# A two-layer transformer step: the MLP up-projection by seven block products per pair of tiles, in place of eight

## The chip, the cores and the metric

The kernel runs on one core of one Trainium2 chip, with fp32 data split into two fp32r parts. The metric is the device time of one launch in microseconds (us). TensorE (PE) multiplies, VectorE (DVE), ScalarE (ACT) and GpSimd (POOL) do the elementwise work, and all transfers are issued in order by SyncE (SP).

## The reference

Two layers (DEPTH 2) work on 128 context and 512 latent tokens of width 1024; the kernel lays them out as 640 token columns. Cut to what matters here:

```python
mod = silu(cvec) @ w_ada[l] + b_ada[l]            # 6144 wide: sh1, sc1, g1, sh2, sc2, g2
h = x * (1 + sc1) + sh1
...                                               # three branches, gated merge, w_out
x = layer_norm(ALPHA * x + g1 * mixed, ln1_g, ln1_b)
h = x * (1 + sc2) + sh2
f = square(relu(h @ w_up[l])) @ w_down[l]         # 1024 -> 4096 -> 1024
x = layer_norm(ALPHA * x + g2 * f, ln2_g, ln2_b)
```

## The kernel before

The program is recorded in Python order and then placed on each engine's queue by a scheduler at build time; each queue runs in order. All matrix products are made of 128x128 weights and 320 or 256 moving columns. For precision each operand is a pair (hi, lo), and each product has three matmuls: hi·hi, hi·lo, lo·hi. `split` makes the pair: ScalarE copies x to hi (L241), VectorE takes lo = x - hi (L242).

The MLP (`mlp`) has 32 up tiles of 128 hidden columns in four pieces (pc) of eight. `fm_blocks` loads the 1024x128 weight of a tile as two halves of 128x512, splits them into a ring of three hi and three lo buffers (`WB`), and `mm_fm` (L163) makes 2 token halves x 8 k-blocks x 3 = 48 matmuls of 128x320 of them. The results go through ReLU (L1212) and square (L1213) and are split again. Then the piece's eight tiles are multiplied into the 1024 outputs (`mm_tm`, L207, four column blocks of 120 matmuls of 128x256, added up in five y tiles at L1243). Hidden tiles of even and odd pieces lie in two sets of sixteen buffers (`even16`, `odd16`). The last piece first scales y by g2 (L1206, GpSimd) and adds ALPHA·x (L1207).

The modulation vector is made in 12 blocks (cb) of 512 columns per layer by `ada_block`: eight weight loads of 256 KB, each multiplied into two accumulators (`acc`), then four matmuls that sum over partitions (L319), a bias and a trip through DRAM (`modd`). Blocks 0 to 3 are sh1 and sc1, 4 and 5 are g1, 6 to 9 are sh2 and sc2, 10 and 11 are g2. `ada_in` does it with two weight buffers and two accumulators in the buffers `F6` and `qs`, with the second accumulator's work on ScalarE and GpSimd (L306, L308); `ada` does it on VectorE alone (L312). In layer 0, blocks 6 to 9 run by `ada_in` beside the gates and merges (`gates`, `merge_a`, `merge_b`, `merge_c`; L163 into `br`); blocks 10 and 11 and all twelve of layer 1 run by `ada` in the MLP of layer 0. Layer 1 has no such work. After the merges comes `out_proj` (L207 again, from `wout`).

## Time and profile before

| | |
|---|---|
| runs | 2985.76 us median of 3 (2978.71 to 2990.69) |
| profiled execution | 2984.24 us, span 2982.3 us |
| TensorE busy | 2790.9 us, 94% of the span, 21248 matmul records |
| VectorE, ScalarE, GpSimd busy | 1958.2, 1366.9, 680.4 us |
| mean granted TensorE clock | 0.956 of full speed |

The profiled execution lasts 1.9 us longer than its span, which begins with its first instruction. Stretches are told by times from the span's start: the MLP of layer 0 runs from about 1048 to 1530 us, that of layer 1 from about 2518 to 2971 us.

### The profile page before, as it was taken

The numbers are of one execution on the slowest core, as the hardware profiler recorded it, in microseconds if no ns is written. First come the engines' busy times: TensorE is split into PE (matmuls) and PEld (weight loads), VectorE is DVE, ScalarE is ACT, GpSimd is POOL, SyncE is SP. The second block draws the span as 40 slices with busy tenths as digits, with TensorE's granted clock in tenths as the row PEclk, the third lists the DMA queues.
The fourth block names the chain that finished last, engine by engine and source line by source line (L and its number), as shares of the span: only waits on it lengthen the run. The fifth ranks groups of instructions, "written<-read, shape, count | busy, mean of one in ns | idle before, by whom it ended". The sixth has DMA issues, their size and how long they took to land.

```text
span 2982.3 us, 56431 instructions
## 1 busy us (share of the span) xinstructions
PE 2790.9 (94%) x21248; PEld 2529.0 (85%) x21248; DVE 1958.2 (66%) x3824; ACT 1366.9 (46%) x3206; POOL 680.4 (23%) x869
## 2 busy tenths in 40 slices
PE   7989989999978999999989899799999899999998
PEld 5979877887868889999989788687878798999998
DVE  4686877877776776777474878878676466223346
ACT  3445665565652343332344456655655424342332
POOL 3241271312233300001040312713121014000011
PEclk8989989999989999999999899899999999999999
DMA  7534323343478244545235433333433762222242
GB/s 261 183 109 118 100 85 92 98 111 87 122 251 260 96 146 148 151 148 184 93 112 154 115 113 95 101 95 93 115 90 91 229 225 89 71 75 75 75 132 85
DMA packets 331255, 378.37 MB, mean 127 GB/s; under 512 B 158111, under 2 KB 180119, under 8 KB 330983
## 3 DMA queue, kind: packets, MB, share of 16 engines
q1 hardware_dynamic: 330983, 374.77, 41.1%
q8 instruction: 167, 2.74, 0.4%
q14 instruction: 105, 0.86, 0.1%
HBM read 306.83 MB, written 67.83 MB: 126 GB/s over the span
## 4 chain that ended last, share of the span: by engine, by line
PE 62%; DVE 15%; DMA 11%; ACT 5%; issue 4%; SPq 2%; POOL 1%; DVEq 0%; ACTq 0%; POOLq 0%
PE tm L207 17%; PE fm L163 16%; PE gl L163 7%; PE br L163 3%; PE tm L233 2%; PE uA L163 2%; PE g L820 2%; DVE Pm L861 2%; DVE T L862 2%; SPq L125 2%; PE st L974 1%; PE xp L939 1%; DVE lo L242 1%; PE ada L319 1%; PE tx L928 1%
## 5 line engine op out<-in xcount | busy, mean ns | idle before, releaser
L242 DVE TENSOR_TENSOR lo<-raw,hi 128x512 fp32r<-128x512 f32 x514 | 383.6, 748 | 401.2 <-ACT hi L241 395.2
L163 PE MATMUL fm<-h,hi 128*128 128x320 f32 (+1 forms) x2720 | 614.6, 315 | 13.3 <-ACT h L391 10.1
L241 ACT ACTIVATE hi<-raw 128x512 fp32r<-128x512 f32 x514 | 323.0, 630 | 612.2 <-PE tm L207 311.8
L163 PEld LDWEIGHTS fm<-h,hi 128*128 128x128 f32 x2720 | 462.7, 192 | 32.1 <-issue 11.2
L163 PE MATMUL fm<-h,lo 128*128 128x320 f32 (+2 forms) x1360 | 421.0, 315 | 9.0 <-DVE lo L242 9.0
L163 PE MATMUL gl<-h,hi 128*128 128x320 f32 x1536 | 379.2, 325 | 2.7 <-ACT f L1002 2.7
L163 PEld LDWEIGHTS gl<-h,hi 128*128 128x128 f32 x1536 | 266.2, 193 | 22.1 <-issue 11.0
L163 PEld LDWEIGHTS fm<-h,lo 128*128 128x128 f32 x1360 | 259.1, 192 | 13.6 <-DVE lo L242 10.2
L163 PE MATMUL gl<-h,lo 128*128 128x320 f32 x768 | 249.1, 325 | 1.8 <-DVE lo L242 1.8
L861 DVE TENSOR_TENSOR Pm<-T,ab 120x341 f32<-120x341 f32 (+30 forms) x434 | 174.2, 401 | 9.1
L862 DVE TENSOR_TENSOR T<-T,Pm 120x341 f32<-120x341 f32 (+30 forms) x434 | 172.8, 398 | 9.4
L312 DVE SCALAR_TENSOR_TENSOR acc<-P,c_sg,acc 128x512 f32<-128x512 f32 x196 | 142.9, 770 | 44.8 <-DMA P<-in_wada_dram 43.5
L1206 POOL TENSOR_TENSOR X<-X,e 128x512 f32<-128x512 f32 x8 | 11.5, 1442 | 680.3 <-DMA e<-modd 355.8
L207 PE MATMUL tm<-hi,h 128*128 128x256 f32 x800 | 160.3, 294 | 0.0
L163 PEld LDWEIGHTS gl<-h,lo 128*128 128x128 f32 x768 | 148.1, 193 | 8.6 <-issue 2.3
L163 PE MATMUL br<-h,hi 128*128 128x320 f32 x512 | 125.9, 334 | 19.7 <-DVE Q L1037 8.2
L207 PEld LDWEIGHTS tm<-hi,h 128*128 128x128 f32 x800 | 130.2, 196 | 5.2 <-issue 1.6
L978 ACT ACTIVATE q1k<-st,edge 64x64 f32<-64x64 f32 x320 | 98.6, 308 | 72.7 <-PE st L974 66.7
L207 PE MATMUL tm<-hi,L 128*128 128x256 f32 x720 | 131.8, 283 | 0.0
L537 POOL TENSOR_TENSOR P<-P,Q 128x512 f32<-128x512 f32 x64 | 84.2, 1316 | 170.9 <-PE o L535 66.8
L207 PE MATMUL tm<-lo,h 128*128 128x256 f32 x400 | 116.7, 292 | 4.5 <-DVE lo L242 4.5
L163 PEld LDWEIGHTS br<-h,hi 128*128 128x128 f32 x512 | 91.3, 201 | 31.2 <-issue 15.8
(554 smaller groups left out, 6899.0 us busy)
## 6 DMA issues: line engine op xcount, KB each, us to landing
raw<-in_win_f_dram SPq DMA_DIRECT2D x172, 256.0 KB
raw<-in_wup_dram SPq DMA_DIRECT2D x128, 256.0 KB
raw<-in_wdn_dram SPq DMA_DIRECT2D x128, 256.0 KB
P<-in_wada_dram SPq DMA_DIRECT2D x114, 256.0 KB
w<-rk SPq DMA_DIRECT2D x48, 321.5 KB
...
```

The costliest lines, as they stand in the source:

```text
L125: self.nc.sync.dma_start(out=out, in_=in_)
L163: nc.tensor.matmul(ps.at(h), w[:, c], ps.of(h, x), start=(k == 0 and p == 0), stop=(k == n - 1 and p == 2))
L207: nc.tensor.matmul(out[t], x[:, ts], w[:, c], start=(k == 0 and p == 0 and (alone or t < 2)), stop=(k == n - 1 and p == 2 and (alone or t ...
L233: nc.tensor.matmul(o, x[:, ts], w[:, c], start=(k == 0 and p == 0), stop=(k == n - 1 and p == 2))
L241: self.nc.scalar.activation(hi, x, AF.Copy)
L242: self.nc.vector.tensor_sub(lo, x, hi.bitcast(F32))
L312: nc.vector.scalar_tensor_tensor(acc[:, s], w, cs[:, k, s:s + 1], acc[:, s], ALU.mult, ALU.add)
L537: nc.gpsimd.tensor_tensor(out=den, in0=den, in1=PT, op=ALU.add)
L820: nc.tensor.matmul(pg[h][:, 128 * j:128 * j + 128], BK[pr, c0 + j].rearrange("p s t -> p (s t)"), RAV[pr, c0 + j, 0:2, :].rearrange("p s t ...
L861: eng.tensor_tensor(out=p, in0=T[:, :, i:i + 1].to_broadcast(sh), in1=Am[:, i, js].unsqueeze(1).to_broadcast(sh), op=ALU.mult)
L862: eng.tensor_tensor(out=T[:, :, js], in0=T[:, :, js], in1=p, op=ALU.add)
L978: nc.scalar.activation(St[kr, s, h, :], p4[kr, s, h, :], AF.Copy, scale=edge[kr, cc:cc + 1])
```

## The change

Tiles 0 to 3 of each layer are made as before. The other 28 are made in 14 pairs (`pair`, `seven`). The product of a pair is seen as a 2x2 block product (two tiles; two halves of k; two halves of the tokens), which is made by seven block products and sums in place of eight. Each block product has 4 k-blocks x 3 = 12 matmuls of 128x320, so 84 for a pair. For it GpSimd takes four differences of weight halves per pair, each of the seven weight operands is split, and VectorE adds the seven results into f0 and f1 out of PSUM. Four sums and differences of blocks of h (`s1` to `s4`) are made and split once per layer by `seven_x`. The lo part of the hidden tiles moves from VectorE to GpSimd (`part`). Hidden tiles lie in a ring of five groups of four buffers, one group a pair (`ring4`): "20 tiles". Weight halves get up to three raw buffers more. One pair of the next piece is made ahead of each piece's output product.

The adaLN blocks 4 to 9 of layer 1 move from the MLP of layer 0 to layer 1's gates and merges (`ada_in`), blocks 10 and 11 of layer 1 to the MLP of layer 1 (`ada`). The scaling of the layer's first norm (`res_tail`) is recorded after pair 2. The scaling of y by g2 is recorded beside pairs 13 to 15.

```diff
+    def ring4(self, n, dt=F32R):
+        n %= 5
+        if n < 3:
+            return [self.K(t, dt)[:, 0:NTOK] for t in K13[4 * n:4 * n + 4]]
...
+    def seven_x(self, g, L, tmp):
...
+        whole(1, 0, nc.vector)
+        whole(0, 0, nc.gpsimd)
+        whole(1, 1, nc.vector)
+        tt((1, 1), (1, 0), (1, 1), ALU.add)
+        parts((1, 1), s1)
+        tt((1, 1), (1, 1), (0, 0), ALU.subtract)
+        parts((1, 1), s2)
+        whole(0, 1, nc.gpsimd)
+        tt((1, 0), (0, 0), (1, 0), ALU.subtract)
+        parts((1, 0), s3)
+        tt((0, 1), (0, 1), (1, 1), ALU.subtract)
+        parts((0, 1), s4)
...
+        def prod(raw, x):
...
+            self.split(raw, hi, lo)
+            ps = bank()[:, 0:HALF]
+            for q in range(4):
+                c = slice(128 * q, 128 * q + 128)
+                for p, (w, i) in enumerate(((hi, 0), (hi, 1), (lo, 0))):
+                    nc.tensor.matmul(ps, w[:, c], x(q, i), start=(q == 0 and p == 0), stop=(q == 3 and p == 2))
...
+        sub = lambda o, a, b: nc.gpsimd.tensor_tensor(out=o, in0=a, in1=b, op=ALU.subtract)
+        add = lambda o, ps, b: nc.vector.tensor_tensor(out=o, in0=ps, in1=b, op=ALU.add)
...
+        nc.scalar.activation(fa, prod(b11, ops["a11"]), AF.Copy)
+        sub(b11, b12, b11)
+        sub(b12, b22, b12)
+        m3 = prod(b22, ops["s4"])
+        sub(b22, b22, b11)
+        add(fb, prod(b22, ops["s2"]), fa)
+        add(ga, m3, fb)
+        add(fa, prod(b21, ops["a12"]), fa)
+        sub(b21, b21, b22)
+        add(gb, prod(b12, ops["s3"]), fb)
+        add(fb, prod(b21, ops["a22"]), gb)
+        last()
+        m5 = prod(b11, ops["s1"])
+        add(ga, m5, ga)
+        add(gb, m5, gb)
...
+            def part(f, hi, lo):
+                nc.scalar.activation(hi, f, AF.Copy)
+                nc.gpsimd.tensor_tensor(out=lo, in0=f, in1=hi.bitcast(F32), op=ALU.subtract)
+
+            def last():
+                nc.scalar.activation(f0, f0, AF.Relu)
+                nc.scalar.activation(f0, f0, AF.Square)
+                part(f0, s[0], s[1])
+
+            self.seven(up(2 * n), up(2 * n + 1), ops, f0, f1, bank, raws, last)
+            nc.vector.scalar_tensor_tensor(f1, f1, 0.0, f1, ALU.max, ALU.mult)
+            part(f1, s[2], s[3])
...
+            while n < 4 * pc + 5 and n < 16:
+                pair(n)
+                if end:
+                    scale(((0, 1), (2, 3), (4,))[n - 13])
+                n += 1
...
-            if l == 0:
...
-                side = self.ada_in([(0, cb) for cb in range(4 + EARLY, 10)], F6[:, 0:2], [F6[:, 2], self.big1("qs", [128, 512])])
...
+            side = self.ada_in([(l, cb) for cb in range(4 if l else 4 + EARLY, 10)], F6[:, 0:2], [F6[:, 2], self.big1("qs", [128, 512])])
...
-            todo = [(0, 10), (0, 11)] if l == 0 else []
...
+            todo = [(l, 10), (l, 11)]
...
-                todo += [(l + 1, cb) for cb in range(12)]
...
+                todo += [(l + 1, cb) for cb in range(4)]
```

ScalarE's queue in an up stage of layer 1, before: L241 with hi<-raw splits a weight half, L1212 and L1213 are ReLU and square of a tile, L241 with L<-f its hi part.

```order
L1212 ACTIVATE f_29973<-fm_29923 128x320
L241 ACTIVATE hi_29987<-raw_29985 128x512
L241 ACTIVATE hi_30049<-raw_30047 128x512
L1212 ACTIVATE f_29973<-fm_29924 128x320
L1213 ACTIVATE f_29973<-f_29973 128x640
L241 ACTIVATE L_29704<-f_29973 128x640
```

ScalarE's queue after, in layer 1 where pair 7 (Q_30437 is its f0, Q_30438 its f1) hands over to pair 8 (f_30586): L321 splits a weight half, L1309, L1310 and L1305 are ReLU, square and hi part, L253 takes the first product of a pair out of PSUM.

```order
L321 ACTIVATE hi_30593<-X_29142 128x512
L321 ACTIVATE hi_30613<-qs_29146 128x512
L1309 ACTIVATE Q_30437<-Q_30437 128x640
L1310 ACTIVATE Q_30437<-Q_30437 128x640
L1305 ACTIVATE ec_30433<-Q_30437 128x640
L253 ACTIVATE f_30586<-u_30597 128x320
L1305 ACTIVATE bon_30435<-Q_30438 128x640
L321 ACTIVATE hi_30631<-qs_29146 128x512
L321 ACTIVATE hi_30650<-raw_30591 128x512
L321 ACTIVATE hi_30669<-F_29144 128x512
```

Where weight halves stood between the ReLUs one or two at a time, the weights of pair 8's third product (hi_30631) now stand behind pair 8's first product and pair 7's last hi part.

GpSimd's queue in layer 1 at the last piece, before: after the first norm's scaling (L1168) nothing stands but the ten scalings of y by g2 (L1206) and then the norm.

```order
L1168 TENSOR_TENSOR y_27661<-y_27661,row_27664 128x512
L1206 TENSOR_TENSOR X_28534<-X_28534,e_32029 128x512
L1206 TENSOR_TENSOR X_28534<-X_28534,e_32031 128x512
L1206 TENSOR_TENSOR BK_28535<-BK_28535,e_32031 128x512
...
L1206 TENSOR_TENSOR y_28537<-y_28537,e_32032 128x512
L290 TENSOR_SCALAR rsd_33072<-mv_33070 128x1
```

The same place after: L249 are the weight differences (the first three and the fourth of pair 13, then those of pair 14), L1341 the scalings, L1306 the lo parts.

```order
L249 TENSOR_TENSOR raw_32558<-raw_32560,raw_32558 128x512
L249 TENSOR_TENSOR raw_32560<-raw_32560,qs_29146 128x512
L1341 TENSOR_TENSOR X_29142<-X_29142,e_32545 128x512
L1341 TENSOR_TENSOR X_29142<-X_29142,w_32546 128x512
L1341 TENSOR_TENSOR X_29142<-X_29142,w_32547 128x512
L1341 TENSOR_TENSOR BK_29143<-BK_29143,w_32547 128x512
...
L1341 TENSOR_TENSOR y_29145<-y_29145,Ld_32548 128x512
L249 TENSOR_TENSOR raw_32562<-raw_32562,raw_32560 128x512
L249 TENSOR_TENSOR X_29142<-F_29144,X_29142 128x512
```

All ten scalings now stand between the third and the fourth weight difference of pair 13.

SP's queue at the end of layer 1's merges, before: Q<-part and P<-gate are the last loads of the merges, wout the weights of the product after them.

```order
L125 DMA Q_27489<-part_3_209 128x640
L125 DMA P_27506<-gate_20_194 128x640
L125 DMA raw_27694<-in_wout_dram 128x512
L125 DMA Q_27566<-part_4_210 128x640
L125 DMA P_27536<-gate_21_195 128x640
```

The same place after, with F and qs the two weight buffers of the adaLN blocks.

```order
L129 DMA raw_27995<-in_wout_dram 128x512
L129 DMA qs_24909<-in_wada_dram 128x512
L129 DMA F_24908<-in_wada_dram 128x512
L129 DMA qs_24909<-in_wada_dram 128x512
L129 DMA F_24908<-in_wada_dram 128x512
L129 DMA qs_24909<-in_wada_dram 128x512
L129 DMA F_24908<-in_bada_r_dram 1x512 x2
L129 DMA qs_27795<-in_ln_b_dram 128x512
L129 DMA Q_27699<-part_4_210 128x640
L129 DMA Q_27704<-part_5_211 128x640
```

The loads of part tiles 4 to 7 now stand behind the last weights of the sixth adaLN block.

## Rows read from the trace of the kernel before

**Rows 1.** The page's parts 1 and 2: busy time, slices of the span.
```profile
PE 2790.9 (94%) x21248; PEld 2529.0 (85%) x21248; DVE 1958.2 (66%) x3824; ACT 1366.9 (46%) x3206; POOL 680.4 (23%) x869
...
PEclk8989989999989999999999899899999999999999
DMA  7534323343478244545235433333433762222242
```
**Rows 2.** Windows, L163 alone: stretch, length, PE and PEld busy, clock, DMA share, GB/s.
```profile
2626.00:2682.30 56.30, 56.30 (x384) 56.21 (x384) 1.00 0.22 71
...
2852.80:2914.00 61.20, 58.12 (x384) 57.72 (x384) 0.97 0.35 108
```
**Rows 3.** Groups by form, 2620 to 2800 us: busy us, mean ns, idle before.
```profile
L242 DVE TENSOR_TENSOR lo<-raw,hi 128x512 fp32r<-128x512 f32 x51 | 35.3, 692 | 102.6 <-ACT hi L241 102.6
L241 ACT ACTIVATE hi<-raw 128x512 fp32r<-128x512 f32 x51 | 32.3, 633 | 80.5 <-PE tm L207 49.9 <-PE fm L163 30.7
L1212 ACT ACTIVATE f<-fm 128x320 f32<-128x320 f32 x32 | 13.7, 430 | 27.6 <-PE fm L163 27.6
L1213 ACT ACTIVATE f<-f 128x640 f32<-128x640 f32 x16 | 11.8, 738 | 0.5
L242 DVE TENSOR_TENSOR L<-f,L 128x640 fp32r<-128x640 f32 x6 | 5.0, 825 | 7.1 <-ACT L L241 7.1
```
**Rows 4.** Groups by form, GpSimd, whole span.
```profile
L537 POOL TENSOR_TENSOR P<-P,Q 128x512 f32<-128x512 f32 x64 | 84.2, 1316 | 170.9 <-PE o L535 66.8 <-ACT Q L532 53.8 <-ACT f L1002 21.1
...
L1057 POOL TENSOR_TENSOR f<-f,Q 128x640 f32<-128x640 f32 x16 | 28.4, 1788 | 65.1 <-DVE Q L1037 43.3 <-DMA f<-part 21.7
```
**Rows 5.** Line L1037, VectorE from PSUM: duration ns min/median/max, first and last start.
```profile
L1037 DVE SCALAR_TENSOR_TENSOR Q<-Q,br x32: 471/484/489, 891.7 to 2411.0; 128x320 f32<-128x320 f32 x32
```
**Rows 6.** Timeline of GpSimd, 1403 to 1409.5 us: start, length, what.
```profile
1404.88 1.73 POOL L1206 TENSOR_TENSOR BK<-BK,e 128x512 f32<-128x512 f32 x1
1406.58 1.75 POOL L1206 TENSOR_TENSOR F<-F,e 128x512 f32<-128x512 f32 x1
```
**Rows 7.** Timeline of VectorE, 1403 to 1412.6 us.
```profile
1405.39 3.48 DVE L242 TENSOR_TENSOR lo<-raw,hi 128x512 fp32r<-128x512 f32 x2
1408.79 1.78 DVE L312 SCALAR_TENSOR_TENSOR acc<-P,c_sg,acc 128x512 f32<-128x512 f32 x1
...
1411.94 0.41 DVE L1243 TENSOR_TENSOR X<-tm,X 128x256 f32<-128x256 f32 x1
```
**Rows 8.** Timeline of TensorE, 1224 to 1229 us.
```profile
1224.98 1.02 PE L319 MATMUL ada<-acc,c_blk 128*1 128x512 f32 x2
1225.93 0.56 PE L163 MATMUL fm<-h,hi 128*128 128x320 f32 x2
```
**Rows 9.** Timelines of ScalarE and TensorE: one place in layer 0 and in layer 1.
```profile
780.69 0.44 ACT L990 ACTIVATE so<-fs 64x64 f32<-64x64 f32 x2
...
2272.86 0.44 ACT L990 ACTIVATE so<-fs 64x64 f32<-64x64 f32 x2
...
964.97 0.36 PE L207 MATMUL tm<-hi,e 128*128 128x256 f32 x1 [0.33 <-DVE P L1037]
...
2437.31 0.28 PE L207 MATMUL tm<-hi,e 128*128 128x256 f32 x1
```
**Rows 10.** Issues of the adaLN weights, 795 to 940 us: ns min/median/max, first and last.
```profile
L125 SPq DMA_DIRECT2D qs<-in_wada_dram x16: 328/333/447, 800.7 to 920.9; - x16
```
**Rows 11.** Windows, all engines: PE, PEld, DVE, ACT, POOL, clock, DMA share, GB/s.
```profile
900.00:965.00 65.00, 56.70 (x360) 53.41 (x358) 41.21 (x67) 17.23 (x27) 24.94 (x15) 0.97 0.84 264
```
**Rows 12.** Timelines at the start of layer 1's MLP: VectorE, TensorE.
```profile
2518.55 3.01 DVE L392 TENSOR_TENSOR h<-f,h 128x512 fp32r<-128x512 f32 x2
...
2542.47 0.31 PE L163 MATMUL fm<-h,lo 128*128 128x320 f32 x1
```
**Rows 13.** Last piece of layer 0: the chain that ended last; TensorE's timeline.
```profile
1399.09 4.59 DMA e<-modd
...
1423.62 0.63 PE L163 MATMUL fm<-h,lo 128*128 128x320 f32 x1 [4.02 <-DVE lo L242]
```

More of the change, by code (lines that the diff above doesn't have):

```diff
@@ L1160, in res_end, with res_tail @@
             self.res_norm(r, t, hT, sb, dst)
-        if hT is None:
-            return
+        if hT is not None and r.which:
+            self.res_tail(r, dst)
+    def res_tail(self, r, dst):
+        nc = self.nc
         for t in range(NT):
@@ L1173, in out_proj @@
         r = self.res_start(l, 0, xsrc)
-        self.res_rows(r, xsrc)
+        L, b = self.L([128, 4, 512]), self.big.tile([128, 2, 512], F32, tag="ab", name=self.nm("row"))
+        self.res_rows(r, [L[:, i] for i in range(4)] + [b[:, 0], b[:, 1], r.more[0], r.more[2]],
+                      ((0, "m"), (1, "m"), ("ln1", "_g"), ("ln1", "_b")))
         for t in range(NT):
@@ new lines, in mlp, with raws, bank @@
+        NP_ = 4
+        hid = {}
+        up = lambda i: a["wup"][l, i].rearrange("p k c -> p (k c)")
+        ntile = [lambda: self.w.tile([128, 512], F32, tag="raw", name=self.nm("raw"), bufs=RAWB)] * 3
+        r, turn = None, [0, 0]
+        def raws():
+            turn[0] += 1
+            kinds = ntile + [(lambda x: lambda: x)(x) for x in (r.more if r else before.more[1:2])]
+            return kinds[turn[0] % len(kinds)]()
+        def bank():
+            turn[1] = (turn[1] + 1) % 6
+            return (self.bank(turn[1], "u") if turn[1] < 4 else (self.D, self.Sp)[turn[1] - 4]("u"))
@@ new lines, in done, with pair @@
+        def done(f, hi, lo):
+            nc.scalar.activation(f, f, AF.Square)
+            self.split(f, hi, lo)
+        def pair(n):
+            s = self.ring4(n)
+            f0, f1 = (self.K("fQ"[n % 2])[:, 0:NTOK] for _ in range(2))
+            def part(f, hi, lo):
[8 more added lines that the diff above has]
+            part(f1, s[2], s[3])
+            hid[2 * n], hid[2 * n + 1] = (s[0], s[1]), (s[2], s[3])
+            self.steps(side, 1)
@@ new lines, in mlp, with scale @@
+        pair(2)
+        self.res_tail(before, xsrc)
+        r = self.res_start(l, 1, xsrc)
+        turn[0] = 0
+        n = 3
+        def scale(ts):
+            for t in ts:
+                for x, yh, h in self.res_x(r, t):
+                    nc.gpsimd.tensor_tensor(out=yh, in0=yh, in1=r.g[0 if t == 0 else 1][h], op=ALU.mult)
+                    nc.vector.scalar_tensor_tensor(yh, x, ALPHA, yh, ALU.mult, ALU.add)
+        for pc in range(NP_):
+            end = pc == NP_ - 1
+            while n < 4 * pc + 5 and n < 16:
[3 more added lines that the diff above has]
+                n += 1
+            xs = [hid.pop(8 * pc + i) for i in range(8)]
+            if end:
+                L = self.L([128, 7, 512])
+                self.res_rows(r, [L[:, i] for i in range(4)], (("ln2", "_g"), ("ln2", "_b")))
@@ L1244, in mlp @@
                 self.steps(side, 3)
-        return hN and hN[1]
+            if pc == NP_ - 2:
+                for _ in side:
+                    pass
+                self.res_rows(r, [x[:, 0:512] for x in self.ring4(16, F32)], ((0, "m"), (1, "m")))
+        return hN
     def ada_first(self, g, wt):
```

133 lines of the change are left out of this document (76 added, 57 removed).

## The prediction

> **What bounds it now.** I read the page's busy shares first. TensorE is busy for 94% of the span, the next engine, VectorE, for 66%, and the granted clock is at its upper level in most slices [rows 1]. So fewer matmuls can pay, unless TensorE then waits. The second view is the windows of the up stages. A stage of eight tiles in layer 1 has 384 matmuls in 56.30 us at clock 1.00 with TensorE busy throughout [rows 2], so a matmul costs 56.30/384 = 146.6 ns. The exception is the last stage, 61.20 us, at 0.97. Third, the groups by form in these stages say how long one instruction takes and what it waits for: ScalarE's and VectorE's weight splits wait for TensorE and for each other [rows 3], so the other engines have slack there. Fourth, the timelines of GpSimd and VectorE, since the change puts much on GpSimd while VectorE works. Last, the merges of both layers, where layer 1 now gets six adaLN blocks: DMA is at 0.84 of its time in layer 0's [rows 11].
>
> **The change, part by part.** The sum is made against the profiled execution, 2984.2 us, which is 1.5 us under the median.
>
> *Matmuls removed.* 28 pairs x 12 = 336 matmuls x 146.6 ns = **-49.3 us**, if TensorE stays as dense as in [rows 2].
>
> *adaLN in the MLPs.* A block ends with four matmuls of 512 columns in TensorE's queue. In the timeline two of them put off the next matmul by 0.95 us (1224.98 to 1225.93) [rows 8], so a block costs 1.90. Eight blocks net of layer 1 leave layer 0's MLP, -15.2, and two run in layer 1's, +3.8: **-11.4 us**.
>
> *adaLN in layer 1's merges.* Layer 0 has four blocks there, layer 1 none. One ScalarE instruction ahead of the merges lies 1492.17 us apart in the two layers, the first matmul of the output projection 1472.34 [rows 9]: four blocks cost 19.8 us, 5.0 each. Six would cost 30 by that. But the weight stream has its own pace: half of the 32 loads of the four blocks, those into qs, go out from 800.7 to 920.9 [rows 10], so a block takes 30 us with two buffers. Layer 1's stream would begin at 800.7 + 1492.2 = 2292.9 and end six blocks later, at about 2473. In SP's queue the loads of part 4 to 7 now stand behind its last weights. An issue there that waits for a buffer holds all behind it, the parts, then the merges, then the second half of the output projection, which began 60 matmuls of 256 columns after 2437.3 (at 146.6 x 256/320 = 117 ns, 7 us), so at 2444. With a landing of 4.59 us, as the e row of [rows 13], and a merge addition of 1.8 on GpSimd [rows 4] it would begin at about 2480. I take **+36 us**. Below, TensorE's own share is four blocks' 19.8, so 20; above, all six run into the DMA share of [rows 11] and 36 grows by half a block more, 52.
>
> *The hand-off from pair to pair.* A product is 12 x 146.6 = 1.76 us and a pair 12.3. There are three hi and three lo buffers, so at the end T0 of a pair the next one's products 1 and 2 lie ready and the third product's split has just got its buffers. TensorE starts it at 3.52 and wants lo two matmuls later, at 3.8. ScalarE's queue has ahead of this split the copy of the new pair's first product, which is there at 1.76 (0.43 like L1212 [rows 3], ends 2.19), and f1's hi part (0.74 like L1213, 2.93). VectorE has had two PSUM additions of 0.48 [rows 5] and the 640-wide square, 0.83, by then. The split's hi ends at 3.56 (0.63), its lo at 4.25 (0.69): 0.4 us late. At 2.93 GpSimd also starts f1's lo part (640 wide, 1.79 alone [rows 4]), which VectorE's lo meets.
>
> What such a meeting costs I read where both engines work on SBUF at once. GpSimd's scalings come every 1.70 us (1404.88, 1406.58) [rows 6], against 1.32 alone for another operation of this form [rows 4], and VectorE's subtractions take 3.48 for two and 1.78 for one [rows 7], against 0.69 [rows 3]. So one of each passes in about 1.70, in lock-step. VectorE's operations with an input in PSUM show nothing of it: 0.41 [rows 7], and 471 to 489 ns over 32 [rows 5]. With the meeting lo ends at 5.0 to 5.3, 1.2 to 1.5 us late. 20 hand-offs have no output product between: 20 x 1.3 = 26, and 8 others at 0.25, **+28 us**. Below: 20 x 0.4 = 8. Above: VectorE never gets ahead in a pair (rival D), 66.
>
> Within a pair GpSimd has four differences and two lo parts. In lock-step that is 6 x 1.70 and 2 x 0.27 for the extra width, and the two VectorE operations left over (0.69 + 0.83) bring it to about 12.2 us, beside TensorE's 12.3. So a pair just fits, with nothing to catch up by.
>
> The Trainium skill, "SBUF — State Buffer", section "Who interferes with whom", says that VectorE with two SBUF inputs and GpSimd take a shared pair of ports for a whole instruction and the other waits in full. The trace agrees that they take turns, but not on the size: by the rule one of each takes 0.69 + 1.32 = 2.01, not 1.70. By it the sum of this case would be rival C's.
>
> *The start of seven products.* VectorE ends the ordinary parts of h at 2518.55 + 3.01 = 2521.56, TensorE ends tile 3 at about 2542.6 [rows 12]. Between, VectorE now has `seven_x` and the first splits: 22 operations of 640 columns x 0.825, three of 0.69, seven more of about 0.69 for adaLN: some 25 us, so to 2546.6. TensorE, with 14 matmuls more at hand, is ready at 2544.7: 2 us. The next lo parts stand behind four or five such operations each, about 2 more, and meetings with GpSimd add 3: 7 a layer, **+14 us**. Below 3 a layer, 6; above 15, if all 640-wide ones meet GpSimd, 30.
>
> *The last piece.* All ten scalings by g2 stand on GpSimd between the third and fourth weight difference of pair 13. They need the output product before, whose sums end y, and rows of g2 that come by DMA (4.59 us [rows 13]), then 10 x 1.3 to 1.70 = 13 to 17. TensorE has five products, 8.8 us, until it needs the fourth difference, whose weights are ready at about T0 + 19: 10 us of waiting, and some 3 of low clock behind it, since the clock fell to 0.97 over the last stage with a smaller gap [rows 2]. 12 to 13 a layer. Before, the same place cost 61.20 - 56.30 = 4.9 in layer 1 [rows 2], and in layer 0 4.02 of waiting [rows 13], to which I add 2.8 for the clock (my estimate, near the 3 above). Net **+13 us**; below 0, if scalings pass while products are ready, above 25.
>
> Sum: -49.3 - 11.4 + 36 + 28 + 14 + 13 = +30.3, so **3014 us**. All low ends give 2957, all high ends 3097.
>
> **Rivals.**
>
> A, pairs at TensorE's pace. VectorE and GpSimd seldom meet: the scalings and lo parts fall where VectorE works from PSUM. For it: VectorE spends 0.48 on each of eight additions a pair without contention [rows 5]. Against: seven lo's a pair leave it few gaps. With 8, 6 and 9 for the last three terms: -49.3 - 11.4 + 36 + 23 = -1.7, 2982.5. It decides where the wait per hand-off is under 0.6 us. This is the case that ends on the other side, not slower.
>
> B, layer 1's merges hide the stream. Its loads run in the time in which TensorE is busy with the gates, and the part loads wait for little: cost 10 in place of 36, 2988. For it: layer 0 hides all but 5 of a block's 30 us. Against: the 120 us of [rows 10] fill most of the merges already, and two blocks more have no cover.
>
> A and B together: 2956.
>
> C, whole instructions take turns. Then a pair needs on VectorE and GpSimd 4 x 1.32 + 2 x 1.79 + 7 x 0.69 + 0.83 = 14.5 us, 2.2 over TensorE's 12.3, in 20 pairs 44 in place of 28: 3031. Against: the pitch of [rows 6]. It is the page's rule at its full size.
>
> D, VectorE meets GpSimd at every operation. Its part grows by seven times 0.48 (half of 1.70 - 0.69, rounded down) to 15.6 us a pair, 3.3 over: 20 x 3.3 = 66, 3053. For it: the 3.48 for two of [rows 7]. Against: GpSimd's six operations can't meet eight of VectorE's.
>
> **How the numbers follow.** My forecast 3014 has 0.36 (own range 2995 to 3040), A 0.15, B 0.10, A and B 0.17, C 0.12, D 0.10. Half a percent is 15 us, about what a measurement of this kernel can tell from no change. Faster: A and B together, 0.17, and the lower third of A, 0.06: 0.23. The same: B 0.10, the rest of A 0.09, the edge of the forecast 0.04 and of C 0.01: 0.24. Slower: the remaining 0.53. The range is 2957 (all low ends, and the case A and B) to 3065 (D and something above); some 0.08 lie on either side.
>
> **What would show it.** (1) 336 fewer matmuls between the same marks. (2) In windows of layer 1's up stages 84 matmuls per pair in 13.4 to 14.0 us rather than 12.3; TensorE's idle time named after VectorE's lo of the weights, L322, whose mean is well over 692 ns, and GpSimd's L249 over 1.32. If L322 stays at 0.7, A holds. (3) In layer 1 the output projection's second half some 207 us behind the ScalarE instruction of [rows 9] (2480 - 2272.9) instead of 171, with the last adaLN weights issued at about 2470 of before's clock; if it follows at about 181, B holds. (4) One gap of about 10 us within pair 13 of each layer, ended by the fourth difference's split. (5) Gaps of 2 to 7 us in the first pair of each layer. I would be wrong, above all, if the scheduler's order leaves VectorE ahead by a product at hand-offs, or if the merges have more cover than layer 0's suggests.

## The result, and the profile after

The changed kernel takes 3074.48 us in the median of 4 runs (3066.10 to 3081.12), the kernel before 2986.97: ratio 1.0295, 95% interval 1.0262 to 1.0329. I had forecast 3014, with a range to 3065. The profiled execution has a span of 3064.3 us, 82.0 more than before's.

The page's parts 1 and 2 of the changed kernel, as in [rows 1], and from its part 5 the lo parts of the weights:

```profile
PE 2783.4 (91%) x20912; PEld 2507.1 (82%) x20912; DVE 2189.7 (71%) x4068; ACT 1415.5 (46%) x3270; POOL 1023.3 (33%) x1087
...
PEclk9989999999899899999989898899998989999999
DMA  7534333233675232333344333333237752322223
...
L322 DVE TENSOR_TENSOR lo<-raw,hi 128x512 fp32r<-128x512 f32 x498 | 398.8, 804 | 285.4 <-ACT hi L321 280.2
```

The same lo parts on the page of the kernel before, and those of the changed kernel in one up stage of layer 1 (2710.9 to 2768.5):

```profile
L242 DVE TENSOR_TENSOR lo<-raw,hi 128x512 fp32r<-128x512 f32 x514 | 383.6, 748 | 401.2 <-ACT hi L241 395.2
...
L322 DVE TENSOR_TENSOR lo<-raw,hi 128x512 fp32r<-128x512 f32 x14 | 13.7, 988 | 3.5 <-ACT hi L321 3.3
```

TensorE has 336 matmuls fewer, but is busy only 7.5 us less, and 91% of a longer span: its mean granted clock is 0.945, 0.956 before. GpSimd went from 680 to 1023 us, and VectorE's lo's take 804 ns in the mean of the whole program (748 before), and 988 in the up stage (692 in [rows 3]), as I had said they would. Where the 82 us lie, by the first matmul of each stage in both traces:

| stretch | before | after | difference |
|---|---|---|---|
| up to layer 0's output projection | 965.0 | 955.1 | -9.8 |
| layer 0: output projection and MLP | 568.8 | 578.6 | +9.8 |
| layer 1 up to its output projection's end | 963.2 | 1020.7 | +57.4 |
| layer 1: MLP to the span's end | 485.3 | 510.0 | +24.7 |

The first stretch has no changed instruction; in all the kernels of this document it lasts from 955 to 973 us, so some 10 us of such a table are chance. The windows of layer 1's up stages after (columns as in [rows 11]): three pairs, four, four, three.

```profile
2606.20:2654.40 48.20, 44.37 (x257) 39.57 (x257) 42.03 (x60) 22.27 (x37) 23.62 (x14) 0.94 0.33 98
2710.90:2768.50 57.60, 54.40 (x343) 50.95 (x342) 42.10 (x59) 28.55 (x50) 30.03 (x19) 0.97 0.25 77
2825.00:2884.50 59.50, 54.41 (x338) 52.29 (x337) 41.93 (x61) 27.64 (x46) 30.50 (x19) 0.94 0.24 75
2941.80:2995.60 53.80, 42.58 (x255) 39.80 (x255) 40.17 (x51) 18.70 (x32) 35.48 (x23) 0.94 0.31 102
```

336 matmuls at the pace of [rows 2] are 49.3 us; four pairs took 57.6 and 59.5, longer than the 384 matmuls of eight tiles had (56.30). No engine is full: VectorE has 42 of 57.6 us, GpSimd 30. At a hand-off, the timelines of TensorE, ScalarE, VectorE and GpSimd:

```profile
2757.82 0.56 PE L246 MATMUL u<-L,hi 128*128 128x320 f32 x2 [1.69 <-ACT hi L321]
...
2755.18 0.42 ACT L253 ACTIVATE f<-u 128x320 f32<-128x320 f32 x1
2756.51 0.74 ACT L1305 ACTIVATE bon<-Q 128x640 fp32r<-128x640 f32 x1 [0.91 <-DVE Q L1314]
2757.15 0.61 ACT L321 ACTIVATE hi<-qs 128x512 fp32r<-128x512 f32 x1
...
2755.18 1.29 DVE L1314 SCALAR_TENSOR_TENSOR Q<-Q 128x640 f32<-128x640 f32 x1
2757.80 0.69 DVE L322 TENSOR_TENSOR lo<-qs,hi 128x512 fp32r<-128x512 f32 x1 [1.32 <-ACT hi L321]
2758.40 2.05 DVE L322 TENSOR_TENSOR lo<-raw,hi 128x512 fp32r<-128x512 f32 x1
2760.38 0.68 DVE L322 TENSOR_TENSOR lo<-F,hi 128x512 fp32r<-128x512 f32 x1
...
2754.49 1.30 POOL L249 TENSOR_TENSOR qs<-qs,X 128x512 f32<-128x512 f32 x1 [0.69 <-DVE lo L322]
2755.74 2.12 POOL L1306 TENSOR_TENSOR bon<-Q,ec 128x640 fp32r<-128x640 f32 x1
2757.83 2.08 POOL L1306 TENSOR_TENSOR Y<-Q,bon 128x640 fp32r<-128x640 f32 x1
```

TensorE waits 1.69 us for the third product's hi, which stands behind f1's hi on ScalarE, which waits 0.91 for VectorE's square of f1; that takes 1.29 instead of 0.83, since it began while GpSimd's difference ran, and ends 0.68 after it. (Both read their inputs from SBUF, the on-chip memory that the engines share.) A lo of VectorE that meets GpSimd's next lo part takes 2.05, the one behind it 0.68. This looks like my hand-off, and I took it for the cause at first.

In layer 1's merges, ScalarE's mark of [rows 9], the issues by SP, and TensorE's timeline:

```profile
2284.17 0.44 ACT L1070 ACTIVATE so<-fs 64x64 f32<-64x64 f32 x2
...
L129 SPq DMA_DIRECT2D qs<-in_wada_dram x24: 327/333/1546, 2300.2 to 2480.4; - x24
L129 SPq DMA_DIRECT2D Q<-part x8: 320/366/434, 2437.2 to 2494.2; - x8
...
2484.21 1.87 PE L399 MATMUL ada<-F,c_blk 128*1 128x512 f32 x2 [13.66 <-DVE F L392]
2488.31 0.58 PE L287 MATMUL tm<-hi,w 128*128 128x256 f32 x1
2491.50 0.39 PE L287 MATMUL tm<-hi,ec 128*128 128x256 f32 x1 [2.25 <-ACT ec L1154]
2494.38 0.58 PE L287 MATMUL tm<-hi,e 128*128 128x256 f32 x1 [0.71 <-DVE P L1117]
```

The last weights go out 196.2 us behind the mark (my 200), the last parts behind them. The product's first matmul that reads a tile of its second half (ec) comes at 207.3 (my 207), and from its 19th matmul, at 210.2, it runs on. The window of the wait, and that of the product behind it up to its 240th matmul (34.7 us; before, the first 240 took 28.3 in all):

```profile
2470.00:2488.30 18.30, 4.64 (x10) 0.80 (x8) 10.44 (x10) 6.31 (x9) 9.41 (x7) 0.65 0.48 141
2488.30:2523.00 34.70, 31.38 (x233) 30.59 (x233) 23.29 (x47) 10.39 (x16) 0.00 (x0) 0.89 0.51 153
```

### The profile page after: what moved, and what is told of

It reads as the page before. It is cut to its first block, busy times and chain, and to the rows that moved or that the text cites. A ratio compares the mean times of both kernels' runs of the same rounds, so it can differ in the third digit from the quotient of the medians.

```text
span 3064.3 us, 56481 instructions
## 1 busy us (share of the span) xinstructions
PE 2783.4 (91%) x20912; PEld 2507.1 (82%) x20912; DVE 2189.7 (71%) x4068; ACT 1415.5 (46%) x3270; POOL 1023.3 (33%) x1087
## 4 chain that ended last, share of the span: by engine, by line
PE 48%; DVE 23%; DMA 12%; ACT 6%; issue 6%; POOL 3%; SPq 3%; DVEq 0%; ACTq 0%; POOLq 0%
PE tm L287 17%; PE gl L167 6%; PE u L246 5%; DVE lo L322 3%; PE br L167 3%; PE fm L167 3%; SPq L129 3%; DVE T L942 2%; DVE Pm L941 2%; PE tm L313 2%; PE uA L167 2%; PE g L900 2%; DMA F<-in_wada_dram 1%; DMA ab<-ad 1%; ACT hi L321 1%
## 5 line engine op out<-in xcount | busy, mean ns | idle before, releaser
L321 ACT ACTIVATE hi<-raw 128x512 fp32r<-128x512 f32 x498 | 310.5, 628 | 564.6 <-PE tm L287 278.0
L167 PE MATMUL fm<-h,hi 128*128 128x320 f32 (+2 forms) x928 | 221.0, 324 | 9.6 <-ACT h L471 5.4
L246 PE MATMUL u<-h,hi 128*128 128x320 f32 x896 | 211.9, 324 | 11.2 <-ACT hi L321 10.8
L246 PE MATMUL u<-L,hi 128*128 128x320 f32 x672 | 159.0, 324 | 24.8 <-ACT hi L321 24.4
L167 PEld LDWEIGHTS fm<-h,hi 128*128 128x128 f32 x928 | 163.4, 197 | 15.8 <-ACT h L471 6.3
L246 PEld LDWEIGHTS u<-h,hi 128*128 128x128 f32 x896 | 156.9, 198 | 21.2 <-ACT hi L321 18.2
L287 PE MATMUL tm<-hi,e 128*128 128x256 f32 x780 | 153.9, 282 | 0.7 <-DVE P L1117 0.7
L246 PE MATMUL u<-h,lo 128*128 128x320 f32 x448 | 142.7, 325 | 9.0 <-DVE lo L322 8.9
L167 PE MATMUL fm<-h,lo 128*128 128x320 f32 (+2 forms) x464 | 148.7, 322 | 0.6 <-DVE lo L322 0.6
L246 PEld LDWEIGHTS u<-L,hi 128*128 128x128 f32 x672 | 117.8, 198 | 31.9 <-ACT hi L321 31.8
L287 PE MATMUL tm<-hi,RAV 128*128 128x256 f32 x660 | 142.1, 284 | 0.4 <-DVE RAV L1155 0.4
```

Source lines behind the costliest of these rows:

```text
L167: nc.tensor.matmul(ps.at(h), w[:, c], ps.of(h, x), start=(k == 0 and p == 0), stop=(k == n - 1 and p == 2))
L246: nc.tensor.matmul(ps, w[:, c], x(q, i), start=(q == 0 and p == 0), stop=(q == 3 and p == 2))
L287: nc.tensor.matmul(out[t], x[:, ts], w[:, c], start=(k == 0 and p == 0 and (alone or t < 2)), stop=(k == n - 1 and p == 2 and (alone or t ...
L321: self.nc.scalar.activation(hi, x, AF.Copy)
```

## The experiments

Each timed in rounds against the kernel before; a stage is the time from its first matmul to the next stage's. "Middle stages" are the two up stages of four pairs in layer 1 (57.6 and 59.5 in the changed kernel).

**e1_ada_back.** The changed kernel, all adaLN blocks of layer 1 back in layer 0's MLP.

```diff
-                self.steps(side, 3)
+                self.steps(side, 9)
...
+            if l == 0:
+                side = self.ada_in([(l, cb) for cb in range(4 + EARLY, 10)], F6[:, 0:2], [F6[:, 2], self.big1("qs", [128, 512])])
...
-            todo = [(l, 10), (l, 11)]
+            todo = [(0, 10), (0, 11)] if l == 0 else []
...
-                todo += [(l + 1, cb) for cb in range(4)]
+                todo += [(l + 1, cb) for cb in range(12)]
```

> The changed kernel with layer 1's adaLN blocks 4 to 11 put back into the MLP of layer 0 (twelve blocks of layer 1 and two of layer 0 there, nine steps of the adaLN generator per column block of an output product in place of three so that they fit; layer 1's merges and MLP have none). Theory M (the merges' weight stream cost most of the loss): the output projection of layer 1 begins about 165 us behind the ScalarE instruction of rows 9, as before, not 204; 49 to 55 us come back there, 8 x 1.9 = 15 are given to TensorE in layer 0's MLP and 4 taken from layer 1's, so the kernel is 35 to 45 us faster than the changed one, at 3030 to 3040. Rival V: VectorE, which makes a block's sums, is so near its limit beside the pairs that the eight blocks (16 x 0.7 to 0.8 us each) lengthen layer 0's MLP by 40 or more, and the whole stays within 10 us of 3074.

Measured: 3069.88, ratio 1.0272 [1.0248, 1.0295]. Layer 1's merges lose their 59 us (1020.7 to 961.7), and layer 0's output projection and MLP go from 578.6 to 643.7. V holds: the second up stage of layer 0 there, VectorE's busy time being the third,

```profile
1191.60:1278.30 86.70, 65.83 (x336) 58.10 (x335) 77.53 (x104) 27.43 (x47) 32.52 (x20) 0.82 0.39 115
...
L392 DVE SCALAR_TENSOR_TENSOR acc<-P,c_sg,acc 128x512 f32<-128x512 f32 x41 | 41.4, 1040 | 2.4 <-DMA P<-in_wada_dram 2.4
```

has VectorE at 77.5 of 86.7 us, 41.4 of it adaLN sums at 1.04 us each. Layer 1, now without adaLN, still takes 55.5 and 56.5 in its middle stages, both at clock 1.00 (0.97 and 0.94 in the changed kernel). The first:

```profile
2724.70:2780.20 55.50, 51.75 (x338) 49.30 (x337) 39.71 (x57) 28.36 (x50) 30.42 (x19) 1.00 0.24 78
```

Its whole MLP takes 496.3 us there, 510.0 in the changed kernel with two blocks. This kernel, e1, is the base of e7 to e11, e13 and e14.

**e2_ada_only.** The kernel before with the move alone.

```diff
-            if l == 0:
+            if True:
...
+                side = self.ada_in([(l, cb) for cb in range(4 if l else 4 + EARLY, 10)], F6[:, 0:2], [F6[:, 2], self.big1("qs", [128, 512])])
...
-            todo = [(0, 10), (0, 11)] if l == 0 else []
+            todo = [(l, 10), (l, 11)]
...
-                todo += [(l + 1, cb) for cb in range(12)]
+                todo += [(l + 1, cb) for cb in range(4)]
```

> The kernel before with the move of the adaLN blocks alone: 4 to 9 of layer 1 in layer 1's merges, 10 and 11 in its MLP; up tiles by eight products as before. Theory M: +45 to +55 in and behind layer 1's merges, -11 in the MLPs, so 3015 to 3030, slower by 1.0 to 1.5%. Rival: the wait in the merges is made by something else of the change (the buffers and queues around it), and the move alone costs TensorE's 5 us a block and gets 15 back: 2985 to 3000.

Measured: 3030.21, ratio 1.0139 [1.0113, 1.0164], +44 us: M, at the upper end. Layer 1 to its output projection's end takes 1027.7 (963.2 before), layer 0's output projection and MLP 550.3 (568.8).

**e12_four.** The same with four blocks (4 to 7) in the merges, 8 to 11 in layer 0's MLP.

```diff
+                side = self.ada_in([(l, cb) for cb in (range(4, 8) if l else range(4 + EARLY, 10))], F6[:, 0:2], [F6[:, 2], self.big1("qs", [128, 512])])
...
+                todo += [(l + 1, cb) for cb in (0, 1, 2, 3, 8, 9, 10, 11)]
```

> The kernel before with four adaLN blocks of layer 1 (4 to 7) in layer 1's merges, as many as layer 0 has there; 8 to 11 stay in the MLP of layer 0. e2 with six there and two in the last MLP cost 44. Theory M (the stream of weights has its pace, 30 us a block, and only what ends behind the merges makes the output projection wait): four blocks end some 140 us behind the ScalarE instruction, before the output projection, which waits for none; +20 as in layer 0 by rows 9, -7.6 in the MLP: 2995 to 3002. Rival (each block costs its share wherever it ends, 64/6 = 10.7 us in the merges): 3015 to 3025.

Measured: 3009.01, ratio 1.0056 [1.0034, 1.0078], +16 us to the 2992.92 of the kernel before in this round: M's 2995 to 3002, which are +9 to +16 to the 2985.78 of e2's round, and not the rival's. As M says, the last weights go out early (143 us behind the mark) and the output projection waits for none (59.7 us). From the mark to the product the profiled run takes 190.1 us, 164.5 before: 26 for four blocks, where M had 20. (Another 13 lie ahead of the mark, where none of the blocks runs; e1, without any, has 12 there.) So the wait at the end is only part of the price: blocks that end in time still slow the merges, by some 6 us each.

**e3_lo_dve.** The lo parts of the hidden tiles on VectorE.

```diff
-                nc.gpsimd.tensor_tensor(out=lo, in0=f, in1=hi.bitcast(F32), op=ALU.subtract)
+                nc.vector.tensor_tensor(out=lo, in0=f, in1=hi.bitcast(F32), op=ALU.subtract)
```

> The changed kernel with the lo parts of the paired hidden tiles made by VectorE, as before the change, so that GpSimd has four operations a pair instead of six. Theory H (the hand-off: ScalarE's hi of f1 and VectorE's square of f1 stand ahead of the third product's split): the lo parts were behind the hi that TensorE waits for, and VectorE gets 2 x 0.83 us a pair more, so the pairs of layer 1 still take 14.4 us each, 3065 to 3090. Rival P (GpSimd's port use at the hand-off makes the delay): with f1's lo off GpSimd the split's lo meets nothing, the weight splits of VectorE go from 0.80 to about 0.75 us in the mean, and a pair takes 13.4 or less: 28 x 1.0 or more off, 3045 or less.

Measured: 3056.47, ratio 1.0229 [1.0206, 1.0252]. Middle stages 54.0 and 56.3. 18 us gained where H expected none and P 28 or more: it lies between, so neither theory is enough alone. GpSimd's share matters, and 4.7 and 7.0 us over TensorE's 49.3 remain without the lo parts on it.

**e6_noscale.** Without the scalings (line L1341 deleted).

> The changed kernel without the ten scalings of y by g2 on GpSimd per layer (left out of the computation; the addition of ALPHA x stays). Theory S (the scalings between pair 13's third and fourth weight difference make the waits of 3 and 4 us there): the last pieces lose their 5 to 8 us more than the middle ones have per pair, so 7 to 10 us a layer and 3055 to 3062 in all. Rival: the waits there come from the late rows of pair 13's weights or from the hand-off alone, and the time stays within 5 us of 3074.

Measured: 3049.82, ratio 1.0212 [1.0182, 1.0241]. The last pieces take 45.1 us (54.6 in the changed kernel) in layer 0 and 42.8 (53.8) in layer 1. S holds, and somewhat more than it had said: 9.5 and 11.0, and 3049.82 in all. The changed kernel's two waits there in layer 1, in TensorE's timeline, are gone (e6's longest wait in that piece is 1.7):

```profile
2953.05 0.50 PE L246 MATMUL u<-h,lo 128*128 128x320 f32 x1 [3.03 <-DVE lo L322]
...
2960.20 0.90 PE L246 MATMUL u<-h,hi 128*128 128x320 f32 x2 [4.25 <-ACT hi L321]
```

**e7_ahead.** e1, and in layer 1 the third product with buffers of its own.

```diff
+            if own:
+                hi, lo = self.K("P", F32R)[:, 0:512], self.K("P", F32R)[:, 0:512]
...
-        add(fb, prod(b22, ops["s2"]), fa)
+        add(fb, prod(b22, ops["s2"], own), fa)
```

> The kernel of e1_ada_back (no adaLN in layer 1), and in layer 1 the third product of each pair splits its weights into two buffers of its own (P, free there), so that its split need not wait for the last product of the pair before. Layer 0 stays as in e1 and serves as the control. Theory H (one wait per hand-off, by the split that is queued behind ScalarE's hi of f1): the two middle up stages of layer 1, 55.5 and 56.5 us in e1 for four pairs of 49.3, fall to 51 to 53, the last piece by 2 to 3, the whole by 10 to 14 to about 3057. Rival W (VectorE's and GpSimd's total work sets the pace, so looking one product further ahead only moves the wait): they stay at 55 or more and the whole within 4 us of 3070.

Measured: 3061.42, ratio 1.0253 [1.0226, 1.0280]. Middle stages 53.8 and 52.9 (55.5 and 56.5 in e1), last piece 50.0 against 54.0. The first of them:

```profile
2724.20:2777.90 53.70, 50.17 (x338) 49.22 (x337) 45.90 (x57) 27.22 (x49) 30.44 (x19) 1.00 0.25 84
```

That is nearly H's 51 to 53, and W's 55 or more falls: the same work of GpSimd and VectorE is done in less time with one product more of look-ahead. But 4 us over the 49.3 remain.

**e8_nosub and e10_beside.** e1 without the four weight differences; then with them in layer 1 again, but into a buffer that nothing reads.

```diff
-        sub(b11, b12, b11)
...
+        def sub(o, a, b):
+            if beside:
+                nc.gpsimd.tensor_tensor(out=self.K("P")[:, 0:512], in0=a, in1=b, op=ALU.subtract)
```

> The kernel of e1_ada_back without the four weight differences of each pair on GpSimd (left out of the computation; the undifferenced halves are split and multiplied, so every other instruction stays). Theory W: with two GpSimd operations a pair in place of six, VectorE's lo's of the weights go back to 0.70 us and pairs to 12.5 or less: the middle stages of layer 1 take 49.5 to 51, and in layer 0, where VectorE also makes the adaLN sums, 8 to 12 us less a stage: 3010 to 3035 in all. Theory H: the differences are not in the hand-off's chain, 54 to 56 us remain in layer 1, and 3055 to 3070.

> The kernel of e8_nosub (the undifferenced weight halves are multiplied, so the computation is changed), but in layer 1 GpSimd makes the same four differences of each pair into a spare buffer (P) that nothing reads: its operations and their use of SBUF are there, no weight waits for them. Layer 0 has none, as in e8. Theory O (order: in e8 the pair's third split stood ahead of ScalarE's hi of f1 because it no longer needed a difference; GpSimd's use of SBUF by itself costs little): the middle up stages of layer 1 stay at 49.3 to 51 us as in e8. Theory P (GpSimd and VectorE take turns at SBUF: 16 x 1.30 + 8 x 1.79 on GpSimd and 28 x 0.69 + 4 x 0.83 on VectorE are 57.8 us a stage, what the changed kernel's stage took): they go back to 55 to 57.

Measured: e8 3023.09, ratio 1.0123 [1.0098, 1.0148]; e10 3042.70, ratio 1.0175 [1.0155, 1.0195]. The first middle stage of e8:

```profile
2688.20:2737.50 49.30, 49.30 (x339) 49.28 (x338) 39.65 (x57) 27.92 (x50) 11.36 (x6) 1.00 0.27 88
```

and of e10:

```profile
2703.40:2758.50 55.10, 52.43 (x339) 49.39 (x338) 46.08 (x57) 27.82 (x50) 29.79 (x17) 1.00 0.24 78
```

The second ones take 50.4 and 55.9, the whole MLP of layer 1 473.1 and 496.6 (496.3 in e1). e8 runs at TensorE's pace. In e10 no weight waits for GpSimd, and ScalarE's queue has the third split ahead of f1's hi, so the chain of the hand-off isn't there; the whole loss is, all the same, with VectorE 6.4 us longer busy on as many instructions. P holds, and theory O falls. GpSimd's operations of a pair come in a row around the hand-off; four of one such row of e10, and VectorE's beside them:

```profile
2729.68 1.76 POOL L251 TENSOR_TENSOR P<-raw,qs 128x512 f32<-128x512 f32 x1
2731.40 1.88 POOL L251 TENSOR_TENSOR P<-raw,raw 128x512 f32<-128x512 f32 x1
2733.24 1.72 POOL L251 TENSOR_TENSOR P<-F,X 128x512 f32<-128x512 f32 x1
2734.93 2.01 POOL L1308 TENSOR_TENSOR w<-f,e 128x640 fp32r<-128x640 f32 x1
...
2731.11 1.01 DVE L1316 SCALAR_TENSOR_TENSOR f<-f 128x640 f32<-128x640 f32 x1
2732.05 5.45 DVE L324 TENSOR_TENSOR lo<-raw,hi 128x512 fp32r<-128x512 f32 x3
```

Three lo's that TensorE wants next take 5.45 us there, and one difference of GpSimd goes by every 1.69 to 1.84 us. Between the rows lo's take 0.68 and GpSimd stands idle. (In layer 0, where neither kernel has differences, the output projection and MLP take 612.9 and 614.9 us, 643.7 in e1, beside 14 adaLN blocks in each: the differences cost 30.8 there, 23.2 in layer 1.)

**e11_hi_dve.** e1 with f1's hi on VectorE, which takes the one link out of ScalarE's queue.

```diff
-            part(f1, s[2], s[3])
+            nc.vector.tensor_copy(s[2], f1)
+            nc.gpsimd.tensor_tensor(out=s[3], in0=f1, in1=s[2].bitcast(F32), op=ALU.subtract)
```

> The kernel of e1_ada_back with the hi part of each pair's second tile (f1) copied by VectorE in place of ScalarE, so that ScalarE's queue goes from the copy of the first product straight to the third product's split; the differences stay on GpSimd. Theory O: the wait on ScalarE's hi at each hand-off (1.7 us in e1) falls by the 0.74 of the hi part and the 0.9 that it waited for VectorE, and the middle stages of layer 1, 55.5 and 56.5 in e1, go to 51 to 53. Theory P: the total on SBUF is larger by VectorE's copies, the stages stay at 55 to 58.

Measured: 3085.30, ratio 1.0323 [1.0294, 1.0352]. Middle stages 57.8 and 57.8: longer, not shorter, P's 55 to 58. It doesn't decide against O, for the link was moved and not removed: the copies take 1.48 to 1.74 us each in VectorE's queue, ahead of the third lo, and in the first of the two stages TensorE waits 3.9 us for VectorE's lo's and 0.4 for ScalarE's hi.

**e13_sub_dve.** e1 with the differences on VectorE (`sub` with nc.vector).

> The kernel of e1_ada_back with the four weight differences of each pair on VectorE in place of GpSimd (which keeps the two lo parts). VectorE's work in a pair grows by 4 x 0.69 = 2.8 us, to about 12.3 alone, as much as TensorE's 12.3. Theory P: VectorE and GpSimd meet only at the lo parts, 4 x (8.9 + 2 x 1.3 of delay) fits, and the middle stages of layer 1 take 50 to 52. Theory O: what stands in ScalarE's queue decides; the third split stands ahead of f1's hi in this order too, so 50 to 53 as well. Rival W (VectorE is full): 54 to 57. In layer 0 the adaLN sums come on top of a full VectorE: stages of 86 us or more, and the whole no faster than e1 by more than 10.

Measured: 3058.21, ratio 1.0223 [1.0207, 1.0240]. Middle stages 53.7 and 54.5, at W's lower edge; P's 50 to 52 and O's 50 to 53 are both missed. The first:

```profile
2715.00:2768.70 53.70, 51.55 (x339) 49.33 (x338) 46.51 (x70) 28.06 (x50) 12.07 (x6) 1.00 0.26 83
```

VectorE is busy for 46.5 us of the 53.7, GpSimd for 12.1. So with few meetings left, differences that the weights wait for still cost 4.4 and 5.2 us a stage when they stand in VectorE's queue.

**e14_memset.** e10 with two fills in place of each difference.

```diff
-                nc.gpsimd.tensor_tensor(out=self.K("P")[:, 0:512], in0=a, in1=b, op=ALU.subtract)
+                for _ in range(2):
+                    nc.gpsimd.memset(self.K("P")[:, 0:640], 0.0)
```

> The kernel of e10_beside with each of GpSimd's differences into the spare buffer replaced by two fills of that buffer with zeros (640 wide, no SBUF read); the weights are undifferenced, so the computation is changed as there. Theory P (what costs is that GpSimd and VectorE both read and write SBUF by turns): the fills don't hold VectorE's subtractions up, and layer 1's middle up stages stay at 49.3 to 51 us as in e8, not 55.0 and 55.9 as in e10. Rival Q (a busy GpSimd delays its own lo parts, or the semaphores do it): 53 to 56.

Measured: 3025.03, ratio 1.0114 [1.0075, 1.0153]. The fills did not land in the places meant: with nothing to wait for, they ran in one row of 112, 0.63 us each, from 2586 to 2664, beside layer 1's first three pairs. The middle stages (49.7 and 50.0) have none and show nothing, but these pairs answer the question. Window of them, and some of VectorE's lo's of the weights in it:

```profile
2590.00:2638.00 48.00, 46.60 (x314) 46.07 (x313) 39.93 (x60) 31.36 (x54) 45.84 (x72) 1.00 0.24 76
...
L325 DVE TENSOR_TENSOR lo<-F,hi x4: 675/676/833, 2600.7 to 2619.9; 128x512 fp32r<-128x512 f32 x4
```

and the same four lo's of e10, with differences of GpSimd in their stretch:

```profile
L324 DVE TENSOR_TENSOR lo<-F,hi x4: 685/1170/1769, 2604.5 to 2627.8; 128x512 fp32r<-128x512 f32 x4
```

GpSimd is busy 45.8 of 48 us, the subtractions beside fills take their 0.68 to 0.69, and the first stage takes 86.0 us as in e8 (86.2), not 95.2 as in e10; the whole MLP of layer 1 takes 471.9. Of the 27 lo's of weights in that stage 4 take over 0.9 us in e14, 6 in e8 and 12 in e10; e14's two longest, 2.06 and 2.07, stand beside GpSimd's lo parts, which read SBUF. Here a GpSimd that is busy with fills costs nothing; one that reads SBUF does.

**e9_nosx.** e1 without `seven_x` (its dictionary filled with plain blocks).

> The kernel of e1_ada_back without the sums and differences of blocks of h at the start of each MLP and their splits (left out of the computation; the plain blocks are multiplied in their place). It prices them. My term was 7 us a layer. From the trace (the first four tiles and three pairs take 99.4 us in layer 0 and 92.1 in layer 1 of e1, where 65.1 are matmuls and 16 were over before the change as well) I now expect 8 to 11 us in each layer to go: 3050 to 3055. Rival: the start is bound by the norm's rows and weights as it was before, and under 3 us a layer go.

Measured: 3057.06, ratio 1.0236 [1.0197, 1.0274]. The first stages take 85.9 and 83.3 us against e1's 99.4 and 92.1: 13.5, more than the 8 to 11 expected, and 8.8. The whole, 13 less than e1's between the medians, is just short of what I expected.

**f1, f2_early, f3_later.** Layer 0 by eight products with all its adaLN blocks, layer 1 by pairs with e3 and e7; f1 and f3 with late rows of g2, f3 with pair 2 by eight products too (the diff is f3's; in f1 and f2 the first line is `if l == 0`).

```diff
+            if l == 0 or n == 2:
+                for i in range(2):
+                    wb, ps = self.wsplit(up(2 * n + i)), self.A("fm")
+                    self.mm_fm(ps, wb, hT[1])
...
+            if end:
+                self.res_rows(r, r.more + [self.K("P")[:, 0:512]], ((1, "m"), (0, "m")))
+                scale(range(NT))
```

> Put together: layer 0 by eight products as before with all its adaLN blocks (the ring of 20 tiles stays), layer 1 by pairs without adaLN, with the lo parts of the hidden tiles on VectorE (e3), the third product's own buffers (e7), and the rows of g2 loaded later, into buffers that the last pairs free, so that nine of the ten scalings stand behind the weight differences. By the stages: layer 0 about 0 to -5 against before, layer 1 92 + 2 x 52 + 42 = 238 where before had 246: 2965 to 2985. If the hand-off can't be removed this way, layer 1 takes 258 and the whole 2990 to 3000.

> f1 with the rows of g2 and the scalings as in the changed kernel (between pair 13's differences). If late scalings only move the cost behind the pairs: layer 1's last piece takes 48 us in place of 41.5 and its last output product 57 in place of 65, layer 0 the same by 0 to 4, and the whole stays within 5 us of f1's 2978. If the 65 us have another cause, the whole is 10 slower.

> f1 with pair 2 of layer 1 made by eight products as well, so that the sums and differences of blocks of h have the time of two more plain tiles before the first pair. TensorE gets 12 matmuls more, 1.8 us; of the 8.8 us that e9 showed in layer 1, 5 to 7 should be hidden: the first stage of 444 matmuls, 88.4 us in f1, is 456 long and takes 84 to 86; the whole 2973 to 2976, which is at the edge of what can be told from f1. If the start waits for GpSimd and VectorE by turns all the same, 2978 to 2982.

Measured: f1 2977.87, ratio 0.9973 [0.9959, 0.9987]; f2 2983.43, 0.9981 [0.9962, 1.0000]; f3 2976.97, 0.9950 [0.9928, 0.9972]. The first middle stage of f3:

```profile
2643.20:2693.60 50.40, 49.89 (x339) 49.36 (x338) 42.14 (x63) 26.70 (x48) 18.95 (x13) 1.00 0.28 89
```

Four pairs in 50.4 us; f1's middle stages take 51.0 and 51.6. The lo parts off GpSimd alone left 54.0 and 56.3 (e3), the look-ahead alone 53.8 and 52.9 (e7): it takes both to come within 2.3 of TensorE's 49.3. Late scalings take 6.1 us off the last piece (47.5 in f2, 41.5 in f1) and give 5.7 to the product behind it (59.4, 65.1). f3's first stage takes 86.9 us with 12 matmuls more, a little short of what I expected. f1 and f3 are faster than the kernel before by 0.3 and 0.5%, little but beyond their intervals; between them the runs don't decide.

## Why the prediction was wrong

The side was right, the size was not: +88 us where I had +28 to the median before. By its terms, with what was measured:

- Matmuls, -49.3: all 336 are gone, and in e8 four pairs take exactly 336 x 146.6 ns. Right.
- adaLN in the MLPs, -11.4: beside eight products right to about 4, for e2's layer 0 (output projection and MLP) is 18.5 shorter, its last MLP 3.6 longer. Beside pairs it is not: eight blocks more lengthen e1's layer 0 by 65.1, 8.1 each where I had 1.90, and the two in layer 1's MLP cost 13.7 (510.0 against e1's 496.3). I had priced TensorE's queue alone and, but for seven operations at the start, given VectorE's sums beside the pairs no price.
- Merges, +36 (20 to 52): +57.4 after, 64.5 in e2. The stream's end and the first matmul of the product's second half came within 4 us of my times. Two things were missing. The last block's sum stands in TensorE's queue behind the first eight matmuls of the output projection, so it held nearly the whole product, not its second half (13.66 us, and a clock of 0.65 and 0.89 in the windows above): the product takes 84.3 us, 59.7 before. And blocks cost the merges time even where nothing waits at the end (e12): from the mark to the product's main run 185.9 us pass, 164.5 before. Some 11 us of the 57.4 lie ahead of the mark and are not shown to belong to the move: the mark is as late in e1, which has none.
- Start of seven products, +14: e9 gives 13.5 and 8.8, so 22, within its bounds.
- Last piece, net +13: e6 gives 9.5 and 11.0; less the 6.8 and 4.9 that I took for before, which no run tests, net 9. Near. In layer 1 the waits of 3.03 and 4.25 are the ones that I placed there, shorter than 10, in two parts, with the clock behind them.
- Pair to pair, +28 (8 to 66): this is **the step that failed**. Layer 1's MLP is 24.7 longer in spite of 24.6 of matmuls removed and 3.8 of adaLN added: 45.5 to explain, less 8.8 for the start and 6.1 for the last piece, 30.6 or 2.2 us a pair. Layer 0: 9.8 + 24.6 + 15.2 = 49.6, less 13.5 and 2.7, 33.4 or 2.4 a pair. Together 64, at the upper end, where I had counted 1.3 at 20 hand-offs and 0.25 at 8. Not all of the 64 is the pairs' own: in layer 1 10 of the 30.6 come with the two adaLN blocks, for of their 13.7 only 3.8 are counted above. 8.0 of the 13.7 lie in the first stage, beside 16 of VectorE's sums, and 5.1 in the middle stages, which have none but run at clock 0.97 and 0.94 (1.00 in e1); why the clock is lower there is open, and in layer 0 no run parts the pairs from the six blocks. The direct price of the differences is e8's: 23.2 and 30.8 less than e1 in the two MLPs, 54 (47 between the medians of the two kernels).

Why it failed: I charged one meeting at each hand-off and took the lock-step of [rows 6, 7] for a pitch at which a pair "just fits" otherwise. The lock-step is there: in e10's row one of each goes by in 1.69 to 1.84 us. But the meetings aren't spread over the pair. They come in a row around the hand-off, where the lo's that TensorE wants next take up to 2.05 us one behind the other, and what GpSimd and VectorE have free between the rows doesn't give it back. e8 and e10 show that this alone is enough: without the differences layer 1's MLP takes 473.1 us, with differences that nothing waits for 496.6, in e1 496.3. It isn't the only way to lose the time: e13 and e3, with few meetings or fewer, still lose 4 to 7 us in a stage while weights wait for differences, and e7, with as many meetings, loses 4 when the third product's split has buffers of its own. How the changed kernel's loss divides between the two is not shown.

My expectation for e10 had a simpler account: the times alone of what the two engines do at SBUF in four pairs add up to 57.8 us, "what the changed kernel's stage took". That agreement is chance. The stage's window holds 19 of GpSimd's operations, not 24, for the rest fall into the output product behind it; at clock 1.00 the same stage takes 55.0 to 56.5 (e1, e10); and in the changed kernel's 57.6 us VectorE (but for its operations on PSUM) or GpSimd is at work in only 44.8, both at once in 16.2, counted from the timelines. So no such sum sets the pace.

The Trainium skill, "SBUF — State Buffer", section "SBUF: two separate sides", says that VectorE with two SBUF inputs contends only with a GpSimd operation that reads SBUF, whole instruction for whole instruction. On who meets whom e10 (three lo's in 5.45 us in the row above) and e14 (0.68 beside fills) agree with it. On the size they don't quite: by the times alone one of each would take 2.01 us, and e10's row passes them in 1.69 to 1.84.

Rival A (seldom any meetings) is refuted by the 1.29 and 2.12 at the hand-off and by e10; B (merges hide the stream) by e2; D (VectorE slowed at every operation, 15.6 a pair) overstates it. C (whole instructions take turns, 14.5 a pair), to which I gave 0.12, comes near by its price, since pairs took 13.8 to 14.1 at clock 1.00 and 14.4 and 14.9 in the changed kernel; but its mechanism, both engines by turns through the whole pair, isn't what the timelines show, so that is luck. With what was measured my terms give -49.3 - 11.4 + 57 + 64 + 22 + 9 = +91 against the 82 of the spans; the first stretch's -10 is most of the difference. Since the 64 is what the stretches leave, that this closes proves nothing.
